# Low parts of fifteen weight tiles of the odd layer made during layer 0 and kept in DRAM

## The chip, the cores and the metric

The kernel runs on one core of a Trainium2 chip. The metric is the device time of one execution in microseconds, median of the runs shown. A change of 0.5% is 7.8 us.

## The reference

Two layers work on 1024 latent tokens and 256 context tokens of 1024 channels. Layer 0 runs a pooling mixer beside a gated short convolution, layer 1 a bidirectional RWKV-7 time mixer beside a Conformer convolution. Each layer is a norm with adaLN modulation, one input projection, the two branches, an output projection and a gated residual. What the change touches is layer 1's projection:

```
hc = modulate(xc, norm_o[j], shc, scc)
uc, rc, kc, vc, zcc, p1c, p2c, zdc = jnp.split(hc @ in_o[j], 8, axis=-1)
yc_rwkv, ctx_states = rwkv_branch(uc, rc, kc, vc, *rp, None)
h = modulate(x, norm_o[j], sh, sc)
u, r, k, v, zc, p1, p2, zd = jnp.split(h @ in_o[j], 8, axis=-1)
```

## The kernel before

Products of float32 are made from two parts: the high part is the value cast to fp32r, the low part what the cast leaves. A projection block `dense` of one weight tile (1024 x 128) sums three products (high x low, low x high, high x high) over eight slices of k, that is 24 matmuls for each of three column groups (512 and 512 latent tokens, 256 context tokens); the first matmul of a block already needs the low weights. A weight tile comes from DRAM into `wr`, of which there is one buffer (`wload`, line 294). ACT casts it to `wh` (line 267), POOL subtracts to `wl` (line 268). `wh` and `wl` have two sets of buffers that alternate, so a tile is split while the block before it runs, and the next `wr` is loaded when POOL has finished its subtraction.

`layer_even` works through four rounds (`for i in range(4)`), each for one group of 128 channels. From round 2 on a round has the blocks U (pooled branch, evicted by ACT into `U`), za (into `sza`), g (into `gcs`), Q (read by DVE), cv and zb. POOL does the window sums between `sa` and `sb` (line 668: two of them in round 2, three in round 3, four in round 4), then two multiplications by `pinv` (line 676). In rounds 3 and 4 block za is issued ahead of the third window sum. All instructions of an engine run in the order in which the Python code issues them; here nothing sorts them. After most blocks `ada_on(2)` loads two tiles `wra` on SP and lets DVE form dot products with `cb` (line 628, tile `junk`); that is unrelated work that uses free time of DVE.

`odd_in` makes layer 1's time mixer. Here a planner (`Lists`) writes the order: each generator yields an engine letter with a cost in ns, a third number is the time until the result may be used, and the planner sorts every engine's instructions by its own simulated times. `weights` and `split_w` bring the tiles 37 to 51 of the list `order` (tile 36 is split as in layer 0), `project` runs the blocks, `shift`, `keys` and `prep` turn their results into the scan's operands. Most of that is DVE work: `prep` runs 20 times (lines 1171 to 1224), POOL helps with the sums `both` (line 1061), `kd`, `ar`, `kb`, and with the low weights:

```
yield "A", 950
nc.scalar.copy(hi, raw)
yield "G", 2310
nc.gpsimd.tensor_tensor(out=lo, in0=raw, in1=hi.bitcast(F32), op=ALU.subtract)
free("wr")
```

SP issues nearly all DMAs, in order: a DMA whose buffer isn't free holds up those behind it.

Of the kernel before, what the change touches and what calls it, by code (L numbers as in the profile page):

```python
# [21 lines left out]
NJ = 4  # L22
# [157 lines left out]
class Kern:  # L180
# [134 lines left out]
    def run(self):  # L315
        tc, nc, A = self.tc, self.nc, self.A
        with ExitStack() as es:
            es.enter_context(tc.manual_schedule())
            cp = es.enter_context(tc.tile_pool(name="cp", bufs=1))
            self.cp = cp  # L320
            self.dr = es.enter_context(tc.tile_pool(name="dr", bufs=1, space=DRAM))
            self.vec = cp.tile([128, NV], F32, name="vec")
            self.cstt = cp.tile([128, CST.shape[1]], F32, name="cstt")
            nc.sync.dma_start(out=self.vec, in_=A["vec"])
            nc.sync.dma_start(out=self.cstt, in_=A["cst"])
            self.modo = cp.tile([128, 24, 2], F32, name="modo")
            nc.vector.memset(self.modo, 0.0)
            self.XR = self.dr.tile([8, 128, T], F32, name="XR")
            self.wp = es.enter_context(tc.tile_pool(name="wp", bufs=1))
            self.wit, self.extra = self.wstream(), {}  # L330
            self.act = es.enter_context(tc.tile_pool(name="act", bufs=1))
            s_ctx = ExitStack()
            self.wpb = s_ctx.enter_context(tc.tile_pool(name="wpb", bufs=1, side="right"))
            self.s_actc = s_ctx.enter_context(ExitStack())
            self.actc = self.s_actc.enter_context(tc.tile_pool(name="actc", bufs=1, side="right"))
            self.co = es.enter_context(tc.tile_pool(name="co", bufs=1))
            self.odd_columns()
            self.s_lpw = ExitStack()
            with ExitStack() as s1:
                self.layer_even(s1)  # L340
            if self.stop == "even":
                s_ctx.close()
                return
            with ExitStack() as s2:
                self.odd_in(s2)
            if self.stop == "prep":
                s_ctx.close()
                return
            s_ctx.close()
            self.s_lpw.close()  # L350
            with ExitStack() as s4:
                self.scan(s4)
# [69 lines left out]
    def layer_even(self, es):  # L422
# [208 lines left out]
        more = [(A["ada_o"][m], self.modo[:, m, 0:2 if m < 16 else 1]) for m in range(24)]  # L631
        more += [(A["ada_eg"][m], gsum[:, m]) for m in range(8)]

        def ada_on(n):
            for _ in range(min(n, len(more))):
                a, dst = more.pop(0)
                w = tp2.tile([128, D], F32, tag="wra", name="wra", bufs=2)
                nc.sync.dma_start(out=w, in_=a)
                columns(w, dst)
# [12 lines left out]
        for i in range(4):  # L652
# [60 lines left out]
            pool_mm(i)  # L713
            ada_on(2)
        ada_on(len(more))
        pool_mm(3)
        nc.vector.tensor_tensor(out=mode[:, 16:24, :], in0=mode[:, 16:24, :], in1=gsum, op=ALU.add)
        bo = self.vcol("ada_b_o", 0, 24)
# [165 lines left out]
    def odd_in(self, es):  # L884
# [81 lines left out]
        def split_w(i):  # L966
            yield "R", f"w{(n - i) % 2}"
            p = (self.wp, self.wpb)[(n - i) % 2]
            raw = self.raws.pop(i)
            self.ready[i] = hi, lo = [p.tile([128, 8, 128], F32R, tag=t, name=t) for t in ("wh", "wl")]  # L970
            yield "A", 950
            nc.scalar.copy(hi, raw)
            yield "G", 2310
            nc.gpsimd.tensor_tensor(out=lo, in0=raw, in1=hi.bitcast(F32), op=ALU.subtract)
            free("wr")
            note(("w", i))
        used = [len(self.order) - self.NZ - 3 * NJ]
# [1421 lines left out]
```

## Time and profile before

| what | value |
|---|---|
| runs shown | 1555.4, 1558.96, 1561.5 us; median 1558.96 us |
| profiled execution, its own time | 1569.38 us |
| its span, first to last instruction | 1567.6 us |
| busy share of the span | PE 89%, DVE 64%, POOL 42%, ACT 40% |
| mean granted clock of TensorE | 0.938 |

The profile is one execution, slower by 10.4 us than the median of the runs. Its busy shares are means over stages that differ: layer 0's projections (to about 430 us), its output projection and the norm of layer 1 (to 560 us), the odd layer's first projections and its preparation (to 940 us), then the scan with the Conformer branch and the output.

### The profile page before, as it was taken

The page shows a single profiled execution, that of the slowest core. Times are in us where ns is not written, and L with a number is a line of the kernel's source. Part 1 is how long each engine was busy: PE and PEld are TensorE (multiplying, and loading weights), DVE is VectorE, ACT ScalarE, POOL GpSimd, SP SyncE. Part 2 cuts the span into 40 slices and gives each one's busy share as a digit, 9 for nine tenths or more (in the row PEclk, how much of TensorE's full clock was granted, in tenths as well). Part 3 has the DMA queues.
Part 4 walks back from the last instruction along what each step waited for, and adds up shares of the span by engine and source line. Part 5 has one row for each costly group of instructions (what it writes and reads, how often), then busy time and mean ns, then how long its engine had stood idle before and what let it go on. Part 6 is the DMA issues. An engine that isn't in the chain of part 4 may idle for free. (4 is left out here: it accounts for less than half of the span.)

```text
span 1567.6 us, 32131 instructions
## 1 busy us (share of the span) xinstructions
PE 1393.9 (89%) x12820; PEld 1092.7 (70%) x12820; DVE 1006.2 (64%) x1681; ACT 621.7 (40%) x1242; POOL 662.7 (42%) x925
## 2 busy tenths in 40 slices
PE   6899999999999998987988878898997988886996
PEld 1488888888888786865766656676775766674775
DVE  3746544347513732499999974878497677688567
ACT  2541111111423533445655521343454543557534
POOL 1352424252644532355565522755566246406004
PEclk9999999999999999999999989899998987878999
DMA  7413223222333112244544666655555566674233
GB/s 264 148 65 126 95 89 121 94 81 95 97 132 128 55 44 76 69 139 148 188 135 144 210 215 160 147 164 139 155 142 138 161 158 166 200 236 125 76 94 108
DMA packets 167894, 208.72 MB, mean 133 GB/s; under 512 B 38112, under 2 KB 129632, under 8 KB 167616
## 3 DMA queue, kind: packets, MB, share of 16 engines
q1 hardware_dynamic: 166448, 205.09, 43.4%
q8 instruction: 101, 1.65, 0.5%
q10 hardware_dynamic: 1296, 1.57, 0.3%
q14 instruction: 49, 0.40, 0.1%
HBM read 149.20 MB, written 55.44 MB: 131 GB/s over the span
## 5 line engine op out<-in xcount | busy, mean ns | idle before, releaser
L302 PE MATMUL d<-sx,wh 128*128 128x512 f32 x1152 | 361.6, 395 | 2.5 <-DVE sx L527 1.4
L302 PEld LDWEIGHTS d<-sx,wh 128*128 128x128 f32 x1152 | 217.2, 189 | 53.2 <-POOL sx L397 1.8
L302 PE MATMUL d<-sx,wl 128*128 128x512 f32 x576 | 229.8, 399 | 4.5 <-DVE u L822 2.7
L1396 POOL TENSOR_TENSOR tmp<-X,Bc 128x120 f32<-128x120 f32 (+2 forms) x300 | 122.1, 407 | 204.1 <-DMA Bc<-ED 181.9
L268 POOL TENSOR_TENSOR wl<-wr,wh 128x1024 fp32r<-128x1024 f32 x37 | 95.5, 2582 | 185.7 <-ACT wh L267 176.2
L992 PE MATMUL d<-sx,wh 128*128 128x512 f32 x512 | 167.5, 409 | 0.0
L1936 PE MATMUL d<-sx,wh 128*128 128x512 f32 x384 | 142.5, 439 | 0.0
L1397 POOL TENSOR_TENSOR X<-X,tmp 128x120 f32<-128x120 f32 (+2 forms) x300 | 120.1, 400 | 23.5
L302 PEld LDWEIGHTS d<-sx,wl 128*128 128x128 f32 x576 | 108.9, 189 | 29.7 <-issue 3.3
L628 DVE SCALAR_TENSOR_TENSOR junk<-wra,cb 128x1024 bf16<-128x1024 f32 x56 | 91.5, 1635 | 52.1 <-DMA wra<-in_ada_o 30.5
L992 PEld LDWEIGHTS d<-sx,wh 128*128 128x128 f32 x512 | 102.3, 200 | 23.9 <-issue 2.9
L992 PE MATMUL d<-sx,wl 128*128 128x512 f32 x256 | 116.2, 454 | 0.0
L302 PE MATMUL d<-sc,wh 128*128 128x256 f32 x576 | 104.1, 281 | 0.0
L1936 PE MATMUL d<-sx,wl 128*128 128x512 f32 x192 | 84.1, 438 | 7.4 <-DVE wl L1910 7.4
L1957 DVE SCALAR_TENSOR_TENSOR acc<-hc,vec,acc 128x960 f32<-128x960 f32 (+14 forms) x120 | 89.3, 769 | 1.1
L302 PEld LDWEIGHTS d<-sc,wh 128*128 128x128 f32 x576 | 88.8, 190 | 1.4
L1936 PEld LDWEIGHTS d<-sx,wh 128*128 128x128 f32 x384 | 75.6, 203 | 16.9 <-issue 0.2
L267 ACT CAST wh<-wr 128x1024 fp32r<-128x1024 f32 x37 | 38.7, 1045 | 117.3 <-PE d L302 86.8
L302 PE MATMUL d<-sc,wl 128*128 128x256 f32 x288 | 81.0, 281 | 0.0
L1498 PE MATMUL sc<-w,bk 64*128 64x128 f32 (+1 forms) x640 | 55.9, 313 | 21.7 <-DMA bk<-BKD 14.1
L1498 PEld LDWEIGHTS sc<-w,bk 64*128 64x128 f32 x640 | 47.0, 212 | 30.2 <-issue 24.9
L1512 DVE TENSOR_TENSOR w<-sc,cstb 64x256 f32<-64x256 f32 x80 | 33.8, 422 | 43.1 <-PE sc L1498 26.4
(380 smaller groups left out, 2909.8 us busy)
## 6 DMA issues: line engine op xcount, KB each, us to landing
wr<-in_in_o SPq DMA_DIRECT2D x32, 512.0 KB
wr<-in_in_e SPq DMA_DIRECT2D x24, 512.0 KB
wra<-in_ada_o SPq DMA_DIRECT2D x24, 512.0 KB
BKD<-bk SPq DMA_DIRECT2D x40, 256.0 KB
BTD<-X SPq DMA_DIRECT2D x20, 512.0 KB
bk<-BKD SPq DMA_DIRECT2D x40, 256.0 KB
Bc<-ED SPq DMA_DIRECT2D x20, 512.0 KB
bkt<-BTD SPq DMA_DIRECT2D x40, 256.0 KB
```

Source lines behind the costliest of these rows:

```text
L267: self.nc.scalar.copy(hi, raw)
L268: self.nc.gpsimd.tensor_tensor(out=lo, in0=raw, in1=hi.bitcast(F32), op=ALU.subtract)
L302: self.nc.tensor.matmul(ps[:, :n], lhsT=w[a][:, k, :], rhs=rhs(src, k, b, c0, n), start=(i == 0), stop=(i == len(seq) - 1))
L628: nc.vector.scalar_tensor_tensor(out=junk, in0=w, scalar=1.0, in1=cb[:, s, :], op0=ALU.mult, op1=ALU.mult, accum_out=dst[:, s:s + 1])
L992: nc.tensor.matmul(ps, lhsT=w[a][:, k, :], rhs=rhs(s, k, b, c0, m), start=(q == 0), stop=(q == len(seq) - 1))
L1396: g.tensor_tensor(out=t, in0=X[:, :, j:j + 1].to_broadcast([128, 8, m]), in1=B[:, j, :, j + 1:16] if j < 8 else B2[:, j - 8, :, j - 7:8], ...
L1397: g.tensor_tensor(out=X[:, :, j + 1:16], in0=X[:, :, j + 1:16], in1=t, op=ALU.add)
L1498: nc.tensor.matmul(ps[h][:, d, i, h:h + 1] if ctx else ps[h][:, d, i], lhsT=bk[R[h], c, d, i], rhs=w[R[h], c, d, sl, i, :], start=True, st ...
L1512: nc.vector.tensor_tensor(out=w[o, c, :, 2 * h], in0=ps[h][o, :, :, h], in1=ma[o].unsqueeze(2).to_broadcast([64, 2, 2, 64]), op=ALU.mult)
L1936: nc.tensor.matmul(ps, lhsT=wt(a, k), rhs=rhs("x", k, b, c0, 512), start=(i == 0), stop=(i == len(seq) - 1))
L1957: nc.vector.scalar_tensor_tensor(out=acc[:, o], in0=hc[:, q], scalar=w, in1=acc[:, o], op0=ALU.mult, op1=ALU.add)
```

## The change

With each `ada_on` of layer 0 one more step `low_on` runs. It stores the low part of the last tile to DRAM (`LO`), loads the next of the tiles 37 to 51 of `order` into `lraw` (two buffers), casts it on ACT into `lhi` (one buffer) and subtracts on POOL in place. In `odd_in`, `split_w` then loads `wl` from `LO` on SP and POOL's subtraction is gone. The cast to `wh` stays, and so does the load of the raw tile, so each of the fifteen tiles is now read twice, its low part written once and read once.

```diff
--- before.py
+++ after.py
@@ -325,6 +325,7 @@
             nc.sync.dma_start(out=self.cstt, in_=A["cst"])
             self.modo = cp.tile([128, 24, 2], F32, name="modo")
             nc.vector.memset(self.modo, 0.0)
+            self.LOD = [self.dr.tile([128, 8, 128], F32, name=f"LO{i}") for i in range(3 * NJ + self.NZ - 1)]
             self.XR = self.dr.tile([8, 128, T], F32, name="XR")
             self.wp = es.enter_context(tc.tile_pool(name="wp", bufs=1))
             self.wit, self.extra = self.wstream(), {}
@@ -631,7 +632,24 @@
         more = [(A["ada_o"][m], self.modo[:, m, 0:2 if m < 16 else 1]) for m in range(24)]
         more += [(A["ada_eg"][m], gsum[:, m]) for m in range(8)]
 
+        low, kept = list(range(len(self.order) - len(self.LOD), len(self.order))), []
+
+        def low_on():
+
+            while kept:
+                i, t = kept.pop()
+                nc.sync.dma_start(out=self.LOD[i - len(self.order)], in_=t)
+            if low:
+                i = low.pop(0)
+                raw = tp2.tile([128, 8, 128], F32, tag="lraw", name="lraw", bufs=2)
+                hi = tp2.tile([128, 8, 128], F32R, tag="lhi", name="lhi")
+                nc.sync.dma_start(out=raw, in_=self.order[i])
+                nc.scalar.copy(hi, raw)
+                nc.gpsimd.tensor_tensor(out=raw.bitcast(F32R), in0=raw, in1=hi.bitcast(F32), op=ALU.subtract)
+                kept.append((i, raw))
+
         def ada_on(n):
+            low_on()
             for _ in range(min(n, len(more))):
                 a, dst = more.pop(0)
                 w = tp2.tile([128, D], F32, tag="wra", name="wra", bufs=2)
@@ -713,6 +731,8 @@
             pool_mm(i)
             ada_on(2)
         ada_on(len(more))
+        while low or kept:
+            low_on()
         pool_mm(3)
         nc.vector.tensor_tensor(out=mode[:, 16:24, :], in0=mode[:, 16:24, :], in1=gsum, op=ALU.add)
         bo = self.vcol("ada_b_o", 0, 24)
@@ -968,10 +988,10 @@
             p = (self.wp, self.wpb)[(n - i) % 2]
             raw = self.raws.pop(i)
             self.ready[i] = hi, lo = [p.tile([128, 8, 128], F32R, tag=t, name=t) for t in ("wh", "wl")]
-            yield "A", 950
+            yield "S", 600, 300
+            nc.sync.dma_start(out=lo.bitcast(F32), in_=self.LOD[i - n])
+            yield "A", 950, 3100
             nc.scalar.copy(hi, raw)
-            yield "G", 2310
-            nc.gpsimd.tensor_tensor(out=lo, in0=raw, in1=hi.bitcast(F32), op=ALU.subtract)
             free("wr")
             note(("w", i))
         used = [len(self.order) - self.NZ - 3 * NJ]
```

In the order that results, the rows of POOL in layer 0's round 4 show the first place. Before (`sa` and `sb` are the window sums, `wl` the low weights of the blocks g, then Q and those after it):

```order
L268 TENSOR_TENSOR wl<-wr,wh 128x1024
L668 TENSOR_TENSOR sa<-U 128x1422
L668 TENSOR_TENSOR sb<-sa 128x1420
L268 TENSOR_TENSOR wl<-wr,wh 128x1024
L668 TENSOR_TENSOR sa<-sb 128x1416
L668 TENSOR_TENSOR sb<-sa 128x1408
L676 TENSOR_TENSOR sa<-sb,pinv 128x1024
L676 TENSOR_TENSOR sa<-sb,pinv 128x256
L268 TENSOR_TENSOR wl<-wr,wh 128x1024 x4
```

Now:

```order
L648 TENSOR_TENSOR lraw<-lraw,lhi 128x1024
L686 TENSOR_TENSOR sa<-U 128x1422
L686 TENSOR_TENSOR sb<-sa 128x1420
L268 TENSOR_TENSOR wl<-wr,wh 128x1024
L648 TENSOR_TENSOR lraw<-lraw,lhi 128x1024
L686 TENSOR_TENSOR sa<-sb 128x1416
L686 TENSOR_TENSOR sb<-sa 128x1408
L694 TENSOR_TENSOR sa<-sb,pinv 128x1024
L694 TENSOR_TENSOR sa<-sb,pinv 128x256
L268 TENSOR_TENSOR wl<-wr,wh 128x1024
L648 TENSOR_TENSOR lraw<-lraw,lhi 128x1024
L268 TENSOR_TENSOR wl<-wr,wh 128x1024 x3
```

A subtraction of `lraw` now stands ahead of the first window sum, and another between the low weights of g and the third window sum; the second one follows za's evictions on ACT, since its cast is queued behind them.

The second place is SP in rounds 3 and 4, where the DMAs of a block stand between one `wr` and the next. Before:

```order
L638 DMA wra<-in_ada_o 128x1024 x2
L294 DMA wr<-in_in_e 128x1024
L638 DMA wra<-in_ada_eg 128x1024 x2
L294 DMA wr<-in_in_e 128x1024
L638 DMA wra<-in_ada_eg 128x1024 x2
L294 DMA wr<-in_in_e 128x1024
```

Now:

```order
L294 DMA wr<-in_in_e 128x1024
L641 DMA LO_79<-lraw 128x1024
L646 DMA lraw<-in_in_o 128x1024
L656 DMA wra<-in_ada_eg 128x1024 x2
L294 DMA wr<-in_in_e 128x1024
L641 DMA LO_80<-lraw 128x1024
```

Each `lraw` load comes behind the next block's `wr` and behind a store to `LO`, and ahead of the two `wra`.

The third place is in the odd layer, where POOL's rows around a low part (`ar`, `kb`, `kd`, `both` and `PT` belong to the preparation) were, before:

```order
L1232 TENSOR_TENSOR kb<-kd 128x256
L1061 TENSOR_TENSOR both<-Z_4362 128x1024
L1191 TENSOR_TENSOR kd<-kd,Z_4365 128x512
L1061 TENSOR_TENSOR both<-Z_4362 128x256
L1211 COPY PT<-E 128x4
L1212 COPY PT<-E 128x4
L974 TENSOR_TENSOR wl<-wr,wh 128x1024
L1216 TENSOR_TENSOR ar<-Z_4367,E 128x2x256
L1232 TENSOR_TENSOR kb<-kd 128x256
```

and where SP now has the load in their stead (`BKD`, `ARD`, `BTD` and `BON` are stores of the preparation's results):

```order
L1333 DMA BTD<-X 128x1024
L1266 DMA BON<-kb 128x256
L992 DMA wl<-LO_73 128x1024
L1309 DMA BKD<-bk 512x1x128 x2
L1292 DMA ARD<-ar 64x1024
L1294 DMA ARD<-ar 128x1x256 x2
L1333 DMA BTD<-X 128x1024
L294 DMA wr<-in_in_o 128x1024
```

No row of line 974's subtraction is left on POOL in that layer; SP has fifteen rows `wl<-LO` more, each ahead of stores of the preparation.

## Rows read from the trace of the kernel before

**Rows 1.** Busy time by stretches of the span. Columns: the stretch (us), its length, then for PE, PEld, DVE, ACT and POOL the busy us and the instructions, then PE's granted clock (1.00 is 2.4 GHz), the DMA engines' busy share and GB/s. The first is rounds 1 to 4 of layer 0's projections, the second the odd layer before its preparation steps run, the third and fourth those steps.

```profile
120.00:400.00 280.00, 280.00 (x1431) 234.79 (x1430) 142.60 (x181) 40.80 (x61) 98.31 (x46) 1.00 0.28 98
...
640.00:660.00 20.00, 20.00 (x97) 16.15 (x96) 9.65 (x8) 9.49 (x11) 6.18 (x4) 1.00 0.09 27
...
660.00:880.00 220.00, 183.39 (x1035) 146.32 (x1034) 209.99 (x259) 116.28 (x208) 126.61 (x100) 0.94 0.49 149
...
880.00:940.00 60.00, 46.70 (x252) 36.25 (x251) 46.89 (x68) 22.30 (x43) 23.92 (x22) 0.89 0.72 233
```

**Rows 2.** Who waited for whom on PE from 660 to 880 us: instruction, what released it, us in total, times, longest us.

```profile
PE m L1258 <- DVE Z L1066: 14.2, 4, 7.7
PE m L1241 <- DVE kb L1236: 12.8, 6, 4.1
```

**Rows 3.** Groups of instructions on POOL from 640 to 940 us: line, engine, operation, output<-input, shapes, count | busy us, mean ns of one | idle us of POOL ahead of them and its releasers.

```profile
L974 POOL TENSOR_TENSOR wl<-wr,wh 128x1024 fp32r<-128x1024 f32 x14 | 38.1, 2718 | 25.5 <-ACT wh L972 25.4
...
L1216 POOL TENSOR_TENSOR ar<-Z,E 128x512 f32<-128x512 f32 x16 | 24.2, 1510 | 0.0
```

**Rows 4.** Three DVE lines of the odd layer's preparation by source line: count, then shortest/median/longest duration in ns, first and last start in us, and the shape.

```profile
L1121 DVE TENSOR_TENSOR sq<-sq,ss x4: 1467/1484/2179, 658.3 to 851.1; 128x1280 f32<-128x1280 f32 x4
...
L1173 DVE TENSOR_TENSOR_SCAN thw<-sm,thw x20: 667/675/2820, 670.7 to 914.0; 128x261 f32<-128x261 f32 x20
...
L1223 DVE SCALAR_TENSOR_TENSOR ar<-kkm,E x20: 410/891/2614, 678.6 to 925.5; 128x256 f32<-128x256 f32 x20
```

**Rows 5.** Timeline of DVE, and one row of POOL, at six of the places where a POOL subtraction of line 974 runs: start us, us, engine, line, operation and tiles; in brackets the idle time before it and its releaser.

```profile
658.33 2.18 DVE L1121 TENSOR_TENSOR sq<-sq,ss 128x1280 f32<-128x1280 f32 x1 [1.44 <-ACT sq L1119]
...
670.71 2.77 DVE L1173 TENSOR_TENSOR_SCAN thw<-sm,thw 128x261 f32<-128x261 f32 x1
...
690.92 2.67 POOL L974 TENSOR_TENSOR wl<-wr,wh 128x1024 fp32r<-128x1024 f32 x1
...
691.34 2.82 DVE L1173 TENSOR_TENSOR_SCAN thw<-sm,thw 128x261 f32<-128x261 f32 x1
...
846.05 2.59 DVE L1223 SCALAR_TENSOR_TENSOR ar<-kkm,E 128x256 f32<-128x256 f32 x1
...
861.46 2.61 DVE L1223 SCALAR_TENSOR_TENSOR ar<-kkm,E 128x256 f32<-128x256 f32 x1
...
899.18 2.61 DVE L1223 SCALAR_TENSOR_TENSOR ar<-kkm,E 128x256 f32<-128x256 f32 x1
```

**Rows 6.** Timeline of ACT where block U ends in rounds 2, 3 and 4 (the evictions into U), ACT's next weight cast and its last eviction into sza in round 4; and PE's first matmul with the weights of block Q in round 4. Columns as in rows 5.

```profile
162.51 0.37 ACT L555 COPY U<-d 128x256 f32<-128x256 f32 x1 [2.24 <-PE d L302]
...
248.33 0.37 ACT L555 COPY U<-d 128x256 f32<-128x256 f32 x1 [2.24 <-PE d L302]
...
334.15 0.37 ACT L555 COPY U<-d 128x256 f32<-128x256 f32 x1 [2.24 <-PE d L302]
334.42 1.05 ACT L267 CAST wh<-wr 128x1024 fp32r<-128x1024 f32 x1
...
348.22 0.39 ACT L558 ACTIVATE sza<-d 128x256 f32<-128x256 f32 x1 [2.27 <-PE d L302]
...
361.76 0.39 PE L302 MATMUL d<-sx,wl 128*128 128x512 f32 x1
```

**Rows 7.** Timeline of POOL in round 4, from U's end to the low part of Q's weights.

```profile
334.61 2.56 POOL L668 TENSOR_TENSOR sa<-U 128x1422 f32<-128x1422 f32 x1 [12.81 <-ACT U L555]
337.24 2.56 POOL L668 TENSOR_TENSOR sb<-sa 128x1420 f32<-128x1420 f32 x1
339.75 2.39 POOL L268 TENSOR_TENSOR wl<-wr,wh 128x1024 fp32r<-128x1024 f32 x1
342.10 2.55 POOL L668 TENSOR_TENSOR sa<-sb 128x1416 f32<-128x1416 f32 x1
344.73 3.24 POOL L668 TENSOR_TENSOR sb<-sa 128x1408 f32<-128x1408 f32 x1
348.04 4.94 POOL L676 TENSOR_TENSOR sa<-sb,pinv 128x1024 f32<-128x1024 f32 x2
352.94 3.38 POOL L268 TENSOR_TENSOR wl<-wr,wh 128x1024 fp32r<-128x1024 f32 x1
```

**Rows 8.** Three transfers of 512 KB in a row in round 3: SP's issues of one `wr` and two `wra`, the DVE instruction that waited for the first `wra`, and the GB/s of the 40 slices of 0.25 us from 256 to 266 us.

```profile
256.35 0.33 SPq L294 DMA_DIRECT2D wr<-in_in_e  x1
256.77 0.86 SPq L638 DMA_DIRECT2D wra<-in_ada_o  x2
...
261.45 1.63 DVE L628 SCALAR_TENSOR_TENSOR junk<-wra,cb 128x1024 bf16<-128x1024 f32 x1 [14.59 <-DMA wra<-in_ada_o]
...
GB/s 0 0 0 0 0 213 147 115 311 442 279 279 410 410 410 442 377 361 377 410 410 410 262 180 82 33 0 0 0 0 0 0 0 0 0 0 0 0 0 0
```

**Rows 9.** Round 2: POOL's two multiplications by `pinv` and the low part of g's weights, and PE's first matmul with those weights; last, PE's first matmul with Q's weights in round 3.

```profile
168.24 3.09 POOL L676 TENSOR_TENSOR sa<-sb,pinv 128x1024 f32<-128x1024 f32 x2
171.29 3.39 POOL L268 TENSOR_TENSOR wl<-wr,wh 128x1024 fp32r<-128x1024 f32 x1
...
176.38 0.40 PE L302 MATMUL d<-sx,wl 128*128 128x512 f32 x1
...
275.94 0.39 PE L302 MATMUL d<-sx,wl 128*128 128x512 f32 x1
```

**Rows 10.** From the chain of waits: one load of 512 KB from DRAM late in the odd layer, start us and us.

```profile
930.59 4.34 DMA ex<-GD
```

## Prediction

> **What bounds the kernel now.** I read busy time by stretches first, since the shares of the whole span mix stages. In layer 0's projections PE is busy for all 280 of 280 us at a granted clock of 1.00 [rows 1]: whatever makes PE wait there is added to the time in full. In the odd layer it is the other way round. From 660 to 880 us DVE is busy for 209.99 of 220 us, PE for 183.39 at a clock of 0.94, POOL for 126.61 [rows 1]. Who waited for whom says the same: PE's longest waits are for DVE results, 14.2 us for shifted projections and 12.8 us for `kb` [rows 2]. So DVE sets the pace there.
>
> The next view is the odd layer's DVE work line by line. The same instruction on the same shape takes 667 ns or 2820 ns (line 1173), 410 ns or 2614 ns (line 1223) [rows 4]. A busy DVE is thus partly a blocked DVE, and the timeline shows by what: POOL's subtraction of line 974 starts at 690.92 us and takes 2.67 us, and the DVE scan that starts behind it at 691.34 ends at 694.16, after POOL [rows 5]. The two engines take turns on such instructions. In the odd layer's stretch POOL runs fourteen of these subtractions, 2718 ns each, 38.1 us together [rows 3].
>
> **The change part by part.** *What goes.* Fifteen POOL subtractions leave the odd layer; the first, ahead of 640 us, lies where DVE is not the bound (9.65 of 20 us busy in the stretch that follows) [rows 1] and I price it at nothing. For the other fourteen I subtract each line's shortest duration from the blocked one: 2.77 and 2.82 less 0.67 is 2.10 and 2.15; 2.59, 2.61 and 2.61 less 0.41 is 2.18, 2.20 and 2.20; the smallest is 2.18 less 1.47, 0.71 [rows 4, 5]. Thirteen at 2.1 and one at 0.7 make 28 us of DVE time. What is late next? PE. Its 183 us in a stretch that shrinks from 220 to about 200 would be 92%, so DVE's idle share will grow from the present 4.5%. I take off a fifth: **minus 22 us**. Bounds: 28 if nothing else binds, 10 if PE's order binds soon.
>
> A rule stands beside this. By the Trainium skill, "SBUF — State Buffer", section "Who interferes with whom", the engine that starts second is blocked for the whole instruction of the other; freed of all fourteen subtractions DVE would gain 38 us, and with the losses below the sum would be minus 27 us instead of minus 11. The rows give 2.0 us of the 2.72 on average, since DVE often comes a few tenths after POOL's start, so they decide.
>
> *What the odd layer gets.* Fifteen loads of a low part on SP, 512 KB each. A load of that size took 4.34 us there [rows 10]; ACT's cast stays. A load needs its `wl` buffer, so it waits at the head of SP's queue until PE is done with the block before last. Queued behind it are stores of `BKD`, `ARD` and `BTD`, for whose buffers DVE waits. Then one block runs, 13.7 us on PE at the least (in layer 0's round 4, g runs from just ahead of za's last eviction, 348.22, to 361.76 [rows 6]), so a load that is issued less than 9 us late costs PE nothing. I take 0, because the planner has put it where PE should be done and DVE, not PE, is what lags. Bounds: 0, and 9 us if PE or DVE waits out two whole loads of 4.34 us. Below nothing: the raw tile's next load now waits for ACT alone and may come some us earlier, but nobody waited for it; the gain is 0. The planner also sorts other instructions anew; the nearest row is one mean wait of PE, 14.2 / 4 = 3.6 us [rows 2], which I allow to either side.
>
> *What layer 0 gets.* Fifteen times: a store, a load, a cast of 1.05 us on ACT [rows 6] and a subtraction of 2.4 us on POOL, the duration of its like [rows 7]. SP's order is `wr`, store, `lraw`, two `wra`. Three 512 KB transfers issued in a row from 256.35 us keep the DMA engines moving until about 262.4; the second is in use at 261.45 [rows 8]. So a `lraw` lands about 6.1 us after the `wr` ahead of it is issued, and the loop from one `wr` to the next is 6.1 (landing) + 1.05 (cast) + 2.4 (new subtraction) + 2.4 (`wl`) = 12 us, under the 13.7 us of a block. Where POOL has nothing else to do, PE covers it. Where POOL has the window sums, it doesn't.
>
> Round 4, in the times of the trace: U is evicted at 334.5 [rows 6]. Cast of `lhi` to 335.6, subtraction to 338.0 (before, the first sum started at 334.6 [rows 7]), two sums of 2.56 to 343.2, `wl` of g to 345.6, where the `wr` of Q can be issued. The next `lraw` lands at 351.8; its cast stands behind za's evictions (348.6 [rows 6]) and this landing, and ends at 352.8; subtraction to 355.2. Only now comes the third sum, which before ran at 342.1 [rows 7]. Third and fourth sum, 2.55 and 2.6 to 3.24, to 360.4 or 361.0; `pinv`, 3.09 [rows 9] to 4.94 [rows 7], to 363.5 or 365.9; `wl` of Q, 2.4 to 3.38, to 365.9 or 369.3. PE needs it at 361.76 [rows 6]: a stall of 4.1 to 7.5 us. I take 6, as POOL shares with DVE's `junk` there.
>
> Round 3 is the same with one sum less and starts at 248.7 [rows 6], 85.8 us earlier: `wl` of Q is ready at 277.5 to 280.3, needed at 275.94 [rows 9]. Stall 1.6 to 4.4, I take 2.5. Round 2: U evicted at 162.9 [rows 6], `lhi` to 163.9, subtraction to 166.3, two sums to 171.5, `pinv` 3.09 to 174.6, `wl` of g 2.4 to 3.39 to 177.0 or 178.0, needed at 176.38 [rows 9]. Stall 0.6 to 1.6, I take 1.2. Round 1 has no subtraction ahead of its sum: 0. Together 9.7 us, bounds 6.3 and 13.5. The clock adds to that: from 660 to 880 us PE stood still for 36.6 us, and its 183.39 us of work ran at 0.94 instead of 1.00 [rows 1], some 11 us longer, 0.3 us for each us of standing still. That is dear for three single stalls, so I take 11 in all and 17 (13.5 x 1.3) as the upper bound.
>
> DMA traffic: 30 transfers more in layer 0, where the engines are busy for 0.28 of the time [rows 1]: covered, except in the chains above. DVE's extra blocking there lies beside PE; it has 142.60 of 280 us of work [rows 1].
>
> **Sum.** Minus 22 plus 11 plus 0 is minus 11 us. The profiled execution took 1569.38 us of its own time, so 1558.4; it is 10.4 us over the median of the runs, 1558.96, and the same difference gives **1548 us**. About 0.5%, 7.8 us, is what a measurement of this kernel can tell from no change.
>
> **Rivals.**
> *PE takes over.* In the odd layer PE and DVE wait for each other in a fixed order, and PE's own work might bind as soon as DVE is freer. For it: PE is at 83% with a lowered clock, and 20 of 20 us busy just before [rows 1]. Against it: its waits are for DVE [rows 2]. Then the gain is 10, the losses 11: 1560 us, no change. Chance 0.28.
>
> *The low parts load too late.* SP holds stores behind a `wl` load, or PE waits for it. Against it: about 9 us of slack a block. Price 9 and a third of the gain, 7: minus 11 plus 9 plus 7 is plus 5, 1564 us, still no change. Chance 0.05.
>
> *Layer 0 becomes bound by its weight loop (slower).* The loop of 12 us fits into a block only if `lraw` lands in time. If the five transfers share the engines instead of following one another, it lands with the last, 6.1 + 2 x 1.35 = 8.8 us (1.35 is 512 KB at 390 GB/s, the level in [rows 8]), and one `junk` of 1.2 us ahead of each subtraction makes 15.9 us against 13.7: 2.2 us in each of thirteen blocks, 29 us. Sum minus 22 plus 11 plus 29: 1577 us, slower. It decides from a landing of about 7.8 us on. For it: DVE waited for `wra` 14.59 us at one place [rows 8], so SP has little slack. Against it: in rows 8 the second transfer was in use a microsecond ahead of the third's end, so they do follow one another. Chance 0.13.
>
> That the subtraction isn't taken away is no rival: the order has no such row left in the odd layer.
>
> **How the numbers follow.** My case, 0.52, and 0.02 for more than it, make faster; PE takes over and late loads make no change, 0.28 and 0.05; the weight loop 0.13. Faster 0.54, within 0.5% 0.33, slower 0.13. The range for 8 in 10: at the low end a gain of 28 with losses of 6.3, 1537; at the high end PE's case with a loss of 15 instead of 11, 1565. My case alone is 1537 to 1551.
>
> **What would show it.** Right: DVE's lines 1173 and 1223 (renumbered) keep long cases from other POOL work but their sums shrink; the odd layer's preparation ends some 20 us sooner relative to its start; in layer 0 PE shows two or three waits for `wl`, longest in round 4, about 6 us. Wrong: DVE's idle time grows by as much as its blocked time falls; PE waits for `wl<-LO`; waits for `wl` at every block of layer 0.

## The result and the profile after

The change made the kernel slower. After: 1575.43 us (median of 7, 1567.9 to 1583.01); before, on the same chip: 1560.1 us (median of 7). The ratio is 1.0101, 95% interval 1.0072 to 1.013. 1548 us was forecast, with 1565 as the upper end.

The two halves of the change went opposite ways, and the first view to read is the start of each stage. These are PE's rows of the odd layer's projections (line 1012) and of the scan stage's first projections (line 1956) after the change, by source line: count, shortest/median/longest ns, first and last start in us.

```profile
L1012 PE MATMUL d<-sx,wl x256: 387/394/1004, 651.2 to 941.3; 128*128 128x512 f32 x128
...
L1956 PE MATMUL d<-sx,wl x192: 387/397/796, 951.8 to 1344.6; 128*128 128x512 f32 x192
```

The same two rows before the change start at 608.6 and 937.8 us. Layer 0 and its output projection thus take 42.6 us longer (651.2 against 608.6), and the odd layer's stretch 28.6 us less (300.6 against 329.2). What follows takes 625.7 us against 629.8; over all kernels below that part lies between 621.5 and 634.6 without an edit to it, so I judge by the first two numbers.

Busy time by stretches after the change (columns as in [rows 1]): rounds 1 to 4, a piece of round 4, the odd layer's stretch.

```profile
120.00:400.00 280.00, 251.18 (x1239) 208.97 (x1238) 163.74 (x144) 48.88 (x67) 141.55 (x55) 0.95 0.38 135
360.00:400.00 40.00, 28.00 (x143) 23.69 (x142) 25.81 (x16) 6.51 (x10) 29.77 (x10) 0.89 0.19 66
...
651.20:951.80 300.60, 264.11 (x1472) 207.87 (x1470) 244.45 (x339) 162.06 (x279) 123.41 (x133) 0.97 0.63 195
```

The odd layer's stretch before the change:

```profile
608.60:937.80 329.20, 273.03 (x1472) 214.04 (x1470) 276.08 (x339) 162.02 (x279) 164.57 (x148) 0.94 0.51 156
```

In the odd layer DVE is busy for 31.6 us less (244.45 against 276.08) with the same 339 instructions, and idle for 56 us against 53: 28.6 of the 31.6 us became time. The lines of [rows 4], renumbered, show where it came from; line 1173, now 1193, has no long case any more, and line 1223, now 1243, has a median of 419 ns instead of 891.

```profile
L1193 DVE TENSOR_TENSOR_SCAN thw<-sm,thw x20: 669/674/683, 710.6 to 928.4; 128x261 f32<-128x261 f32 x20
...
L1243 DVE SCALAR_TENSOR_TENSOR ar<-kkm,E x20: 410/419/1508, 716.4 to 938.6; 128x256 f32<-128x256 f32 x20
```

In layer 0 PE is busy for 251 of 280 us, where it was for all of them. PE's waits from 100 to 450 us (what released it: us in total, times, longest):

```profile
PE d L302 <- POOL wl L268: 22.2, 3, 12.0
PE d L302 <- DVE cv L718: 6.7, 3, 3.2
PE a L666 <- DVE y L667: 1.3, 1, 1.3
```

The waits for low weights are one in each of rounds 2, 3 and 4 (3.56, 6.60 and 12.01 us), those for `cv` one in each of rounds 1, 2 and 3 (2.64, 3.25 and 0.77 us). Round 4's chain on POOL, from U to Q's low weights (it answers to [rows 7]):

```profile
360.63 2.46 POOL L648 TENSOR_TENSOR lraw<-lraw,lhi 128x1024 fp32r<-128x1024 f32 x1 [10.44 <-ACT lhi L647]
363.05 3.54 POOL L686 TENSOR_TENSOR sa<-U 128x1422 f32<-128x1422 f32 x1
366.67 3.42 POOL L686 TENSOR_TENSOR sb<-sa 128x1420 f32<-128x1420 f32 x1
370.05 2.40 POOL L268 TENSOR_TENSOR wl<-wr,wh 128x1024 fp32r<-128x1024 f32 x1
380.77 2.40 POOL L648 TENSOR_TENSOR lraw<-lraw,lhi 128x1024 fp32r<-128x1024 f32 x1 [8.32 <-ACT lhi L647]
383.12 3.53 POOL L686 TENSOR_TENSOR sa<-sb 128x1416 f32<-128x1416 f32 x1
386.73 4.01 POOL L686 TENSOR_TENSOR sb<-sa 128x1408 f32<-128x1408 f32 x1
390.82 4.86 POOL L694 TENSOR_TENSOR sa<-sb,pinv 128x1024 f32<-128x1024 f32 x2
395.64 3.31 POOL L268 TENSOR_TENSOR wl<-wr,wh 128x1024 fp32r<-128x1024 f32 x1
```

Beside it on SP, ACT and PE: the `wr` is issued when POOL's `wl` of 370.05 is done, `lraw` behind it lands 7.2 us after that issue, and PE stands until 399.00.

```profile
372.47 0.33 SPq L294 DMA_DIRECT2D wr<-in_in_e  x1
372.85 0.42 SPq L641 DMA_DIRECT2D LO<-lraw  x1
373.32 0.42 SPq L646 DMA_DIRECT2D lraw<-in_in_o  x1
...
379.64 1.05 ACT L647 CAST lhi<-lraw 128x1024 fp32r<-128x1024 f32 x1 [5.96 <-DMA lraw<-in_in_o]
...
399.00 0.80 PE L302 MATMUL d<-sx,wl 128*128 128x512 f32 x1 [12.01 <-POOL wl L268]
```

And DVE's `junk` at the same time, with its group in the page (56 of them, 133.1 us busy, 2376 ns each); behind it the same instruction before the change, its shortest, median and longest duration in ns:

```profile
360.88 3.30 DVE L629 SCALAR_TENSOR_TENSOR junk<-wra,cb 128x1024 bf16<-128x1024 f32 x1
...
364.21 3.46 DVE L629 SCALAR_TENSOR_TENSOR junk<-wra,cb 128x1024 bf16<-128x1024 f32 x1
...
380.93 3.32 DVE L629 SCALAR_TENSOR_TENSOR junk<-wra,cb 128x1024 bf16<-128x1024 f32 x1 [13.25 <-DMA wra<-in_ada_eg]
...
384.29 3.45 DVE L629 SCALAR_TENSOR_TENSOR junk<-wra,cb 128x1024 bf16<-128x1024 f32 x1
```

```profile
L629 DVE SCALAR_TENSOR_TENSOR junk<-wra,cb 128x1024 bf16<-128x1024 f32 x56 | 133.1, 2376 | 89.1 <-DMA wra<-in_ada_o 57.5
...
L628 DVE SCALAR_TENSOR_TENSOR junk<-wra,cb x56: 1215/1226/3383, 122.2 to 382.7; 128x1024 bf16<-128x1024 f32 x56
```

Read the two engines against each other. The `junk` of 360.88 takes 3.30 us instead of 1.23: POOL's subtraction ends at 363.09, and 1.1 us later `junk` ends. POOL's sum is begun at 363.05, needs 2.56 alone and takes 3.54: it gets the place when `junk` ends. They change over like this as long as both have work. The Trainium skill's "SBUF — State Buffer", section "Who interferes with whom", has it so: whoever issues first keeps the shared ports for its whole instruction, and the other is blocked. Here the rows agree for both engines: each instruction ends some 1.1 us (DVE) or 2.4 us (POOL) after the other engine's has ended, so a POOL sum pays about 1.0 us and a `junk` about 2.1.

The clock adds its share: from 360 to 400 us it is granted at 0.89, and the matmul behind the wait takes 0.80 us instead of 0.39, the clock's lower level, 1.2 GHz, instead of 2.4 (from 399 to 402 us it is granted at 0.50). PE's waits in the list add up to 30.2 us, the loss is 42.6. The stretches from the start to the odd layer, before and after, show the rest: PE does as many matmuls, but is busy for 13.1 us more (595.83 against 582.71) at a granted clock of 0.96 instead of 0.99, and idle for 29.5 us more.

```profile
0.00:608.60 608.60, 582.71 (x2835) 463.25 (x2835) 284.42 (x395) 170.98 (x276) 232.99 (x142) 0.99 0.31 105
...
0.00:651.20 651.20, 595.83 (x2834) 472.84 (x2835) 331.46 (x395) 185.19 (x291) 288.02 (x157) 0.96 0.36 123
```

### The profile page after: what moved, and what is told of

Read it like the earlier page. It is cut to its first block, busy times and chain, and to the rows that moved or that the text cites. A ratio compares the mean times of both kernels' runs of the same rounds, so it can differ in the third digit from the quotient of the medians.

```text
span 1577.5 us, 32202 instructions
## 1 busy us (share of the span) xinstructions
PE 1395.0 (88%) x12820; PEld 1094.4 (69%) x12820; DVE 1022.7 (65%) x1681; ACT 636.1 (40%) x1257; POOL 671.1 (43%) x925
## 4 chain that ended last, share of the span: by engine, by line
PE 33%; DVE 15%; DMA 8%; POOL 6%; issue 5%; ACT 5%; SPq 3%; DVEq 0%; ACTq 0%; POOLq 0%
PE d L302 8%; PE d L1956 5%; PE d L1012 4%; PE d L2098 3%; DMA bk<-BKD 2%; POOL X L1417 2%; POOL tmp L1416 2%; DMA Bc<-ED 2%; PE sc L1518 2%; PE d L940 2%; PE pa L1742 1%; PE pa L1737 1%; PE pa L1761 1%; PE po L1732 1%; DVE Z L1086 1%
## 5 line engine op out<-in xcount | busy, mean ns | idle before, releaser
L302 PE MATMUL d<-sx,wh 128*128 128x512 f32 x1152 | 370.6, 404 | 2.5 <-DVE sx L528 1.4
L302 PE MATMUL d<-sx,wl 128*128 128x512 f32 x576 | 236.1, 410 | 33.3 <-POOL wl L268 23.4
L302 PEld LDWEIGHTS d<-sx,wh 128*128 128x128 f32 x1152 | 223.9, 195 | 55.0 <-POOL sx L398 1.8
L1416 POOL TENSOR_TENSOR tmp<-X,Bc 128x120 f32<-128x120 f32 (+2 forms) x300 | 115.7, 386 | 199.8 <-DMA Bc<-ED 177.5
L629 DVE SCALAR_TENSOR_TENSOR junk<-wra,cb 128x1024 bf16<-128x1024 f32 x56 | 133.1, 2376 | 89.1 <-DMA wra<-in_ada_o 57.5
L1012 PE MATMUL d<-sx,wh 128*128 128x512 f32 x512 | 163.7, 401 | 0.0
L302 PEld LDWEIGHTS d<-sx,wl 128*128 128x128 f32 x576 | 112.2, 195 | 61.4 <-POOL wl L268 24.5
L268 POOL TENSOR_TENSOR wl<-wr,wh 128x1024 fp32r<-128x1024 f32 x37 | 105.7, 2857 | 99.8 <-ACT wh L267 90.5
L1956 PE MATMUL d<-sx,wh 128*128 128x512 f32 x384 | 144.1, 444 | 0.0
L1012 PEld LDWEIGHTS d<-sx,wh 128*128 128x128 f32 x512 | 99.0, 193 | 22.0 <-issue 2.4
L1012 PE MATMUL d<-sx,wl 128*128 128x512 f32 x256 | 112.6, 440 | 0.0
L1956 PE MATMUL d<-sx,wl 128*128 128x512 f32 x192 | 85.9, 447 | 9.7 <-DVE wl L1930 9.7
L1956 PEld LDWEIGHTS d<-sx,wh 128*128 128x128 f32 x384 | 77.2, 207 | 17.4
L648 POOL TENSOR_TENSOR lraw<-lraw,lhi 128x1024 fp32r<-128x1024 f32 x15 | 36.6, 2443 | 103.0 <-ACT lhi L647 103.0
```

The lines of the kernel that those rows point to most:

```text
L268: self.nc.gpsimd.tensor_tensor(out=lo, in0=raw, in1=hi.bitcast(F32), op=ALU.subtract)
L302: self.nc.tensor.matmul(ps[:, :n], lhsT=w[a][:, k, :], rhs=rhs(src, k, b, c0, n), start=(i == 0), stop=(i == len(seq) - 1))
L629: nc.vector.scalar_tensor_tensor(out=junk, in0=w, scalar=1.0, in1=cb[:, s, :], op0=ALU.mult, op1=ALU.mult, accum_out=dst[:, s:s + 1])
L648: nc.gpsimd.tensor_tensor(out=raw.bitcast(F32R), in0=raw, in1=hi.bitcast(F32), op=ALU.subtract)
L1012: nc.tensor.matmul(ps, lhsT=w[a][:, k, :], rhs=rhs(s, k, b, c0, m), start=(q == 0), stop=(q == len(seq) - 1))
L1416: g.tensor_tensor(out=t, in0=X[:, :, j:j + 1].to_broadcast([128, 8, m]), in1=B[:, j, :, j + 1:16] if j < 8 else B2[:, j - 8, :, j - 7:8], ...
```

## The experiments

My theory: the halves are independent. The odd layer gains 27 to 29 us since POOL's subtraction no longer blocks DVE; layer 0 loses 42 us since `wr`, landing of `lraw`, cast, subtraction, window sums and low weights form one chain, which is longer than a block where the sums are. Rivals: the traffic itself; POOL's added work alone; for the gain, the planner's new order.

Eleven kernels ran, each beside runs of before on the same chip. In the table "odd from" is the first start of an odd-layer projection in the trace (layer 0 and its output projection), "stretch" from there to the scan's first projection, both in us. Both are of one execution each, and scatter: before and e11_odd_dve, which are alike in layer 0, start at 608.6 and 607.1, and e8_ahead_dve, e10_pool_again and e12_pool_planned, alike there too, at 610.5, 609.1 and 611.9. Differences below 3 us say nothing.

| kernel | odd from | stretch | median us | ratio to before (95%) |
|---|---|---|---|---|
| before | 608.6 | 329.2 | 1560.1 to 1562.5 | 1 |
| after | 651.2 | 300.6 | 1575.4 | 1.0101 (1.0072 to 1.013) |
| e1_odd_only | 610.6 | 302.3 | 1543.0 | 0.9873 (0.9836 to 0.9909) |
| e2_layer0_only | 649.0 | 328.8 | 1601.8 | 1.0239 (1.0204 to 1.0275) |
| e3_split_only | 622.6 | 301.7 | 1550.7 | 0.9925 (0.9894 to 0.9956) |
| e4_dma_only | 606.6 | 302.5 | 1534.1 | 0.9822 (0.9788 to 0.9857) |
| e5_ahead | 621.9 | 301.2 | 1546.0 | 0.9896 (0.9856 to 0.9937) |
| e6_no_junk | 624.6 | 300.5 | 1552.2 | 0.9933 (0.9908 to 0.9959) |
| e8_ahead_dve | 610.5 | 300.4 | 1534.8 | 0.9827 (0.9801 to 0.9853) |
| e9_dve | 610.1 | 302.0 | 1541.3 | 0.9859 (0.981 to 0.9908) |
| e10_pool_again | 609.1 | 329.2 | 1565.6 | 1.0024 (0.9993 to 1.0055) |
| e12_pool_planned | 611.9 | 329.5 | 1564.2 | 1.0 (0.9974 to 1.0025) |
| e11_odd_dve | 607.1 | 311.2 | 1546.2 | 0.9897 (0.9836 to 0.9959) |

### Each half alone

e1_odd_only:

```diff
-            self.LOD = [self.dr.tile([128, 8, 128], F32, name=f"LO{i}") for i in range(3 * NJ + self.NZ - 1)]
+            self.LOD = [self.dr.tile([128, 8, 128], F32, name="LO")] * (3 * NJ + self.NZ - 1)
...
-        low, kept = list(range(len(self.order) - len(self.LOD), len(self.order))), []
+        low, kept = list(range(len(self.order) - len(self.LOD), len(self.order)))[:1], []
```

> The odd layer's part of the change alone: all fifteen loads read one DRAM tile that layer 0 makes once, so layer 0 does one step instead of fifteen (and the low parts of fourteen tiles are another tile's). The theory: the two parts of the change are independent; the trace of after shows the odd layer 28.6 us shorter, so the ratio to before is about 0.982 (1560 to 1532 us), with layer 0 at before's time. A rival, that the odd layer's gain came from its later start or from another alignment: 0.99 to 1.0.

e2_layer0_only (against after):

```diff
-            yield "S", 600, 300
-            nc.sync.dma_start(out=lo.bitcast(F32), in_=self.LOD[i - n])
-            yield "A", 950, 3100
+            yield "A", 950
             nc.scalar.copy(hi, raw)
+            yield "G", 2310
+            nc.gpsimd.tensor_tensor(out=lo, in0=raw, in1=hi.bitcast(F32), op=ALU.subtract)
```

> Layer 0's part of the change alone: the low parts are made and stored as in the change, but the odd layer subtracts on POOL as before. The theory: the first matmul of the odd layer comes 42 us later than before and nothing is gained, ratio 1.025 to 1.028 (1600 to 1603 us). A rival, that part of layer 0's loss is given back by the scan's alignment (the traces had the scan 4 us shorter): 1.02.

The stages came out as expected: stretch 302.3 with layer 0 nearly at its old time, and odd from 649.0 with the old stretch, 328.8. The gain of e1's median is 19 us (1543.0 against 1561.6), less than the trace's 27 in the stretch: the one step left in layer 0 costs a wait for `cv` of 1.7 us, the rest I leave to the scatter. The stretch is 300.4 to 302.5 us in all eight kernels that only load low parts in the odd layer, wherever it starts between 606.6 and 651.2, so the later start is not the cause. The medians add up: minus 1.3% and plus 2.4% make plus 1.1%, the whole has plus 1.0%. e1's interval reaches to 0.9909, so its median alone leaves the rival of 0.99 open; the stretch of 302.3 does not. For e2 the measured 1.0239 lies between theory (1.025) and rival (1.02) and tells little.

### Layer 0: work or traffic

e3_split_only (with the one DRAM tile of e1 and one buffer of `lraw`):

```diff
+        raw0 = tp2.tile([128, 8, 128], F32, name="raw0")
+        nc.sync.dma_start(out=raw0, in_=self.order[low[0]])
...
-                nc.sync.dma_start(out=raw, in_=self.order[i])
-                nc.scalar.copy(hi, raw)
-                nc.gpsimd.tensor_tensor(out=raw.bitcast(F32R), in0=raw, in1=hi.bitcast(F32), op=ALU.subtract)
+                nc.scalar.copy(hi, raw0)
+                nc.gpsimd.tensor_tensor(out=raw.bitcast(F32R), in0=raw0, in1=hi.bitcast(F32), op=ALU.subtract)
```

> The odd layer as in the first run, and in layer 0 the fifteen casts and subtractions without the traffic: they work on one tile that is loaded once, and one store is made. The theory (the chain of load landing, cast, subtraction and low weights is too long only as a whole): without the landing, POOL waits for nothing new; what is left is a late wl of Q in round 4 (3 to 4 us), in round 3 (1 to 2), with some clock: 8 us over the first run. Rival 1, that POOL's added work alone is the cause (with DVE blocking it): 30 to 42 us over the first run. Rival 2, that the traffic alone is the cause: 0 to 2.

e4_dma_only:

```diff
                 nc.sync.dma_start(out=raw, in_=self.order[i])
-                nc.scalar.copy(hi, raw)
-                nc.gpsimd.tensor_tensor(out=raw.bitcast(F32R), in0=raw, in1=hi.bitcast(F32), op=ALU.subtract)
```

> The change whole but for the cast and the subtraction in layer 0: the tiles are loaded and stored as they are (the low parts that the odd layer reads are the raw tiles). The theory: DVE's junk waits longer for wra behind two more transfers, so DVE is late with the evictions of cv in three rounds (6.7 us of waits in the trace of after), with clock 8 us over the first run; no wait for wl. Rival 1 (POOL's work alone): 0 to 2 over the first run. Rival 2 (traffic alone): 30 to 42 over the first run.

The traffic alone costs nothing: odd from 606.6, and rounds 1 to 4 look as before for PE:

```profile
120.00:400.00 280.00, 280.00 (x1432) 234.84 (x1431) 134.54 (x183) 42.23 (x65) 98.97 (x47) 1.00 0.43 152
```

My own expectation of 8 us was wrong there: transfers alone make no late eviction of `cv`. The trace of after shows what does. In round 1, ahead of the first wait for `wl`, POOL's two subtractions, of `lraw` and `wl`, run back to back from 124.04 to 129.77 us and hold two `junk`, which take 3.07 and 3.30 us; in e4 the same two take 1.23 and 1.22. `cv` stands behind them on DVE.

```profile
124.44 3.07 DVE L629 SCALAR_TENSOR_TENSOR junk<-wra,cb 128x1024 bf16<-128x1024 f32 x1 [5.20 <-DMA wra<-in_ada_o]
...
127.56 3.30 DVE L629 SCALAR_TENSOR_TENSOR junk<-wra,cb 128x1024 bf16<-128x1024 f32 x1
```

In rounds 2 and 3 two `junk` are held in the same way; that they also start late there, since `wra` stands on SP behind a `wr` that waits for POOL's `wl`, is likely and not shown apart. The work alone costs 12 us over e1 (622.6 against 610.6) where 8 were expected; by medians 8. Zero and 12 do not make 40: what costs is the two in series.

### Layer 0: landing or blocking

e5_ahead:

```diff
+        got = []
+
+        def fetch():
+            if low:
+                raw = tp2.tile([128, 8, 128], F32, tag="lraw", name="lraw", bufs=3)
+                got.append((low.pop(0), raw))
+                nc.sync.dma_start(out=raw, in_=self.order[got[-1][0]])
+        fetch()
...
-            if low:
-                i = low.pop(0)
-                raw = tp2.tile([128, 8, 128], F32, tag="lraw", name="lraw", bufs=2)
+            fetch()
+            if got:
+                i, raw = got.pop(0)
                 hi = tp2.tile([128, 8, 128], F32R, tag="lhi", name="lhi")
-                nc.sync.dma_start(out=raw, in_=self.order[i])
```

> The change with lraw loaded one step ahead (three buffers instead of two), so that ACT's cast finds its tile in SBUF. The theory: the loss in layer 0 is the chain of landing (6 to 7 us behind the wr), cast, subtraction and low weights in series with the window sums; with the landing taken out what remains is what the run without traffic showed, 12 us over the run of the odd layer alone: the odd layer's first matmul at 622 to 625 us instead of 651, ratio 0.992 to 0.995 (1550 to 1554 us). Rival 1, that DVE's junk beside POOL's subtraction stretches both whatever the landing: 635 us, ratio 1.0. Rival 2, that the loads are not what matters: 651 us, ratio 1.010.

e6_no_junk:

```diff
-            for s in range(dst.shape[1]):
-                nc.vector.scalar_tensor_tensor(out=junk, in0=w, scalar=1.0, in1=cb[:, s, :], op0=ALU.mult,
-                                               op1=ALU.mult, accum_out=dst[:, s:s + 1])
+            nc.vector.memset(w[:, 0:1], 0.0)
```

> The change without DVE's dot products junk (each is one short memset of the loaded wra instead, so DVE still waits for each load; the adaLN sums of layer 1 and of the pooled branch are missing). Theory 1, the landing in series: POOL's instructions get back to 2.40 and 2.56 us, but the waits for landings stay; the loss in layer 0 falls from 42 to about 30 us (odd layer's first matmul at 638). Theory 2, the two engines block each other: in round 4 the chain loses 7 us, so the wait for wl of 12.0 us becomes 5, that of round 3 from 6.6 to 2, the waits for cv go; the loss falls to about 15 us (622), ratio 0.993.

Either edit alone takes 27 to 29 of the 42.6 us away. PE's waits from 100 to 450 us, first e5_ahead, then e6_no_junk:

```profile
PE d L302 <- POOL wl L268: 8.8, 3, 4.2
```

```profile
PE d L302 <- POOL wl L268: 13.3, 4, 6.5
```

In both the waits for `cv` are gone. e6's round 4 on POOL shows the first three sums at 2.54 to 2.56 us where after has 3.42 and more, and the wait for the landing still there:

```profile
347.05 2.55 POOL L684 TENSOR_TENSOR sb<-sa 128x1420 f32<-128x1420 f32 x1
349.56 2.39 POOL L268 TENSOR_TENSOR wl<-wr,wh 128x1024 fp32r<-128x1024 f32 x1
360.33 2.40 POOL L646 TENSOR_TENSOR lraw<-lraw,lhi 128x1024 fp32r<-128x1024 f32 x1 [8.38 <-ACT lhi L645]
```

e6 measured 624.6, near its theory 2 (622) and not theory 1 (638); its longest wait is 6.5, not 5. e5 measured 621.9, its theory's value (its median, 0.9896, is a little better than the 0.992 to 0.995 expected). e5 takes out more than the landing, though: its third sum in round 4 runs at 2.55 us again (3.53 in after), since the subtraction ahead of it no longer meets `junk`.

```profile
358.10 2.55 POOL L694 TENSOR_TENSOR sa<-sb 128x1416 f32<-128x1416 f32 x1
```

Each cause on its own seems to hold two thirds, so together more than the whole. What is counted twice are the waits for `cv` and `y`, 8.0 us, which go in both, and the clock's share; the waits for `wl` fall by 13.4 and by 8.9, which is the 22.2 once. A run with both edits was not made.

The loop itself has no room left. In round 2 of after the `wr` issues come 13.5 to 14.0 us apart (184.70, 198.63, 212.64, 226.16), which is a block's own time, and the rows between two of them show that nothing but the loop sets this: each step waits for the one before it, 7.0 us of landing, the cast, the subtraction and a `wl` of 3.38 us that `junk` holds, and the next `wr` is issued as `wl` ends.

```profile
184.70 0.33 SPq L294 DMA_DIRECT2D wr<-in_in_e  x1
...
191.73 1.05 ACT L647 CAST lhi<-lraw 128x1024 fp32r<-128x1024 f32 x1 [10.14 <-DMA lraw<-in_in_o]
...
192.86 2.39 POOL L648 TENSOR_TENSOR lraw<-lraw,lhi 128x1024 fp32r<-128x1024 f32 x1 [8.19 <-ACT lhi L647]
195.22 3.38 POOL L268 TENSOR_TENSOR wl<-wr,wh 128x1024 fp32r<-128x1024 f32 x1
...
198.63 0.33 SPq L294 DMA_DIRECT2D wr<-in_in_e  x1
```

By these rows the loop only just keeps up with PE.

### Layer 0: another engine

e9_dve (and e8_ahead_dve, the same on top of e5):

```diff
-                nc.gpsimd.tensor_tensor(out=raw.bitcast(F32R), in0=raw, in1=hi.bitcast(F32), op=ALU.subtract)
+                nc.vector.tensor_tensor(out=raw.bitcast(F32R), in0=raw, in1=hi.bitcast(F32), op=ALU.subtract)
```

> Loaded one step ahead as in the run before, and the subtraction of lraw made by DVE instead of POOL. The theory: POOL, whose chain of window sums, pinv and low weights is what PE waits for, has no work more than before the change, and DVE has room in layer 0 (142.60 of 280 us busy before); the waits for wl go but for one of a microsecond, layer 0 loses 0 to 4 us, the odd layer keeps its 27: odd layer's first matmul at 609 to 613 us, ratio 0.985 to 0.990 (1538 to 1546 us), as fast as the odd layer's part alone. Rival: DVE, with a microsecond or two more in each step, is late with Q and cv, and PE waits 2 to 3 us in three rounds: 618 us and over, ratio 0.995.

> The change with the subtraction of lraw on DVE, but loaded as in the change, behind the wr of the same step. It tells whether it is the landing or POOL's chain that has to be mended. If POOL's chain is the whole: as the run before, odd layer's first matmul at 609 to 613 us, ratio 0.985 to 0.990. If DVE, which now waits for each landing ahead of its evictions, passes the delay on: PE waits for Q, cv or y, 615 to 630 us, ratio 0.992 to 1.0. I hold the second for a little likelier, at the low end (616, 0.991).

Both bring layer 0 to 610 us. In e9 the landing is as late as in the change (6.6 to 8.1 us behind the `wr` in rounds 2 to 4, where ACT waited for it), and PE's waits from 100 to 450 us are 2.8 us in all: I had held a delay passed on by DVE for a little likelier (616 us), and it did not come. So POOL's chain was what had to be mended; the landing hurt only as a part of it. Without POOL's subtraction the loop has room: in round 2 of e9 the `wr` issues come 11.2 to 11.8 us apart (177.69, 188.96, 200.12, 211.90). e8's stretches and its DVE group:

```profile
120.00:400.00 280.00, 279.15 (x1418) 233.52 (x1417) 185.42 (x196) 52.21 (x71) 107.26 (x44) 1.00 0.43 154
610.50:910.90 300.40, 263.18 (x1473) 206.98 (x1471) 245.32 (x339) 162.40 (x279) 123.29 (x133) 0.98 0.63 195
```

```profile
L656 DVE TENSOR_TENSOR lraw<-lraw,lhi 128x1024 fp32r<-128x1024 f32 x15 | 33.1, 2208 | 28.7 <-ACT lhi L655 28.7
```

DVE's subtraction takes 2.2 us on average (1.21 at the shortest), but DVE is at 185 of 280 us there. e8 beats both kernels: 1534.8 us, 27.7 us under before's 1562.5.

### The odd layer: POOL's instruction or the planner's order

e10_pool_again and e12_pool_planned (both on e8_ahead_dve):

```diff
             yield "A", 950, 3100
-            nc.scalar.copy(hi, raw)
+            nc.scalar.copy(hi, raw); nc.gpsimd.tensor_tensor(out=raw.bitcast(F32R), in0=raw, in1=hi.bitcast(F32), op=ALU.subtract)
```

> The last but one version (loaded ahead, subtracted by DVE in layer 0), with a subtraction by POOL put back into the odd layer for each of the fifteen tiles; its result goes into the raw tile and is used by nobody. The planner's order of everything else is kept as it is, and the low parts are still loaded. It asks what the odd layer's 27 us are. The theory: they are DVE time that POOL's subtraction takes by blocking DVE, 2.0 us each; then the odd layer's stretch (its first matmul to the scan's first projection) goes back from 300 to 326 to 331 us, ratio 0.998 to 1.002. Rival, that the planner's new order made the gain: it stays at 300 to 306, ratio 0.983 to 0.987.

```diff
-            yield "A", 950, 3100
+            yield "A", 950
             nc.scalar.copy(hi, raw)
+            yield "G", 2310
+            nc.gpsimd.tensor_tensor(out=raw.bitcast(F32R), in0=raw, in1=hi.bitcast(F32), op=ALU.subtract)
```

> The same subtraction without use, but known to the planner with the cost it had before (2310 ns on POOL behind the cast), so that the order may shift too. The theory: the order matters little, 326 to 331 us in the odd layer as in the run before. The rival (order): as before the change, 329 us, with the run before it at 300 to 306.

A subtraction whose result nobody reads takes the whole gain away, 329.2 and 329.5 us, with the planner told or not. The order is not the cause. Both runs also keep `wr` occupied for longer, as before the change; but no projection of the odd layer waited for its weights in the trace of before, so an earlier `wr` is no source of the gain. e10's stretch on the engines, and the group on POOL:

```profile
609.10:938.30 329.20, 274.71 (x1473) 213.87 (x1471) 269.62 (x339) 162.67 (x279) 160.80 (x148) 0.92 0.58 178
```

```profile
L1002 POOL TENSOR_TENSOR wr<-wr,wh 128x1024 fp32r<-128x1024 f32 x15 | 40.6, 2708 | 36.1 <-ACT wh L1002 31.8 <-issue 4.2
```

Fifteen instructions of 2.71 us on POOL lengthen DVE's same 339 instructions by 24 us (269.62 against 245.32), and the stretch by 29. In e10 POOL also stood 31.8 us waiting for the cast, so part of its loss may be later work of POOL's own; e12 has 18.2 of that, and 277.84 us on DVE.

e11_odd_dve (against before):

```diff
-            yield "G", 2310
-            nc.gpsimd.tensor_tensor(out=lo, in0=raw, in1=hi.bitcast(F32), op=ALU.subtract)
+            yield "D", 1150
+            nc.vector.tensor_tensor(out=lo, in0=raw, in1=hi.bitcast(F32), op=ALU.subtract)
```

> The kernel before with one edit: in the odd layer DVE itself makes the low weights instead of POOL; nothing in layer 0, no traffic. DVE, the bound of that stretch, is given 1.21 us more per tile (its shortest subtraction of this shape in layer 0), 17 us for fourteen, and is freed of 28 us of blocking. The theory: the stretch gets shorter by 11 us though its bound has more to do, 318 us, ratio 0.992 to 0.995. Rival, that POOL's work cost DVE less than I think: 329 + 17 = 346 us, ratio 1.01.

```profile
L974 DVE TENSOR_TENSOR wl<-wr,wh 128x1024 fp32r<-128x1024 f32 x15 | 21.5, 1432 | 5.6 <-ACT wh L972 5.6
```

```profile
607.10:918.30 311.20, 267.47 (x1473) 209.56 (x1471) 266.66 (x354) 163.96 (x279) 130.66 (x133) 0.95 0.53 165
```

The bound engine does 21.5 us of added work and is busy for 9.4 us less (266.66 against 276.08); 11 were expected. The stretch shrank by 18 instead of 11: the other 8.6 us are idle time of DVE that went. The largest single change is in DVE's one long wait for POOL's sum `both`, here before and in e11:

```profile
DVE Z L1063 <- POOL both L1061: 7.3, 1, 7.3
...
DVE Z L1063 <- POOL both L1061: 0.5, 1, 0.5
```

Other waits went and came (5.6 us for ACT's cast are new). The planner was given other costs in e11, so its order shifted too; how much of the 8.6 us that makes is not shown.

## Why the prediction was wrong

- **What bounds the kernel** held: DVE in the odd layer, blocked by POOL's subtraction; PE in layer 0, where each wait adds to the time in full.
- **The odd layer's gain** was right in mechanism and a little small: 28.6 us in the profile, 27 in e1, against 22, bounds 10 to 28. The step that failed in it is "I take off a fifth" for PE: DVE's busy time fell by 31.6 us where 28 were forecast, and its idle time hardly grew, 53 to 56 us. The rival "PE takes over" did not come.
- **The loads of low parts** cost 0 as taken; no wait for them shows on PE in the odd layer.
- **Layer 0's stalls** is the step that failed: 11 us, bounded at 17, against 42.6. In round 4 I forecast 4.1 to 7.5 and 12.0 came. From U's last eviction (334.5 before, 359.6 after) Q's weights were to be ready after 31.4 to 34.8 us, and were after 39.35. The first subtraction ended after 3.5 us as forecast. Two sums took 7.0 instead of 5.1. The landing took 7.2 from the `wr` issue instead of 6.1 (6.6 to 7.6 in rounds 2 to 4). The third and fourth sum with `pinv` took 12.5 against 8.3 to 10.7. Rounds 3 and 2 the same: 6.60 and 3.56 against at most 4.4 and 1.6.
- Why these durations were off: I took POOL's rows of before, when `junk` came at other times. Now the two `wra` land just behind `lraw`, so `junk` starts with POOL's subtraction and the engines hold each other through the sums. `junk`'s median is 2950 ns now and was 1226, and without it (e6) the loss falls by 27 us. "DVE's extra blocking there lies beside PE" overlooked that POOL is blocked in turn. The loop of "12 us, under the 13.7 us of a block" is the other step that failed: it measures 13.5 to 14.0, 7.0 instead of 6.1 for the landing and 3.4 instead of 2.4 for `wl`. By itself it made no wait.
- Not foreseen: DVE is late for PE as well. 6.7 us of PE's waits are for `cv`, in three rounds, behind `junk` that POOL's two subtractions hold. They are gone in e3, e4, e5, e6 and e8, each of which leaves out or moves one of three things, POOL's subtraction, the load it waits for or `junk`; e9 has one of 0.7 us.
- The clock: I took 0.3 us for each us of standing still, and thought it dear. PE was busy for 13.1 us more and idle for 29.5 us more, so 0.4.
- **The rival that layer 0 becomes bound by its weight loop** had the sign and, by 2 us, the time; that nearness is luck, since it took 22 us for a gain of 28.6 and 40 for a loss of 42.6. Its place was off too: not 2.2 us in each of thirteen blocks with a landing of 8.8, but three large waits behind the window sums with a landing near 7. Its chance, 0.13, was too low for a loop of 12 against 13.7 us, worked out with the shortest durations.
- The upper end of the range, 1565, is 1564 by its own terms (a gain of 10, a loss of 15, from 1558.96); that changes nothing.

## What to carry to other kernels

A loop that seemed to fit into its cover by 1.7 us did not, since two of its durations were read where less ran beside them: cost each step as it is beside the work that will then stand next to it. Look at what a moved load does to the others in its queue, for they arrive together and start engines that hold each other. And work that is taken off the bound engine's neighbour may go to the engine with room at the other place (DVE in layer 0), not to the one that did it before.

## What the runs showed of the hardware

- POOL and DVE hold each other alternately: 2.56 becomes 3.5 us on POOL and 1.23 becomes 3.3 to 3.5 on DVE at the same time. Handing fifteen POOL instructions of 2.7 us to a DVE that was already the bound made the stretch 18 us shorter (e11).
- Thirty added transfers of 512 KB in layer 0 (DMA busy share 0.43 in e4, 0.28 before [rows 1]) cost no time where no engine worked on what they brought (e4: PE busy for 280.00 of 280 us, odd layer from 606.6 against 608.6).
